# Query heads by way of DRAM, and a top-k search with two small operations a step, in a hybrid attention and mLSTM block

## The chip, the cores and the metric

The kernel runs on one core of a Trainium2 chip. The metric is device time in microseconds (us) from launch to end; lower is better. The engines of a core are TensorE (PE, matrix products), VectorE (DVE), ScalarE (ACT), GpSimd (POOL) and SyncE (SP), which here issues the DMAs. Each engine works through its own instructions in order.

## What is computed

One layer of a streaming encoder on 1024 tokens of width 1024: half a SwiGLU network, then a mixing stage with sparse attention and an mLSTM side by side, then half a second SwiGLU network. The part that the change touches is the attention's indexer (`iq`, `ik`), its top-k and the main queries (`aq`):

```python
h = rms_norm(x, mix_norm[l])
(aq, ak, av, iq, ik, iw, mx, mv, mi, mf, mo, ga, gb) = split_columns(h @ w_in[l])
q = rms_norm(aq.reshape(B, S, ATT_HEADS, ATT_HEAD_DIM), q_norm[l])
...
logits = jnp.einsum('bqhd,bsd->bqhs', iq_blk, ik)
score = jnp.einsum('bqhs,bqh->bqs', jax.nn.relu(logits), iw_blk).astype(jnp.float32) * idx_scale
...
top_s, top_i = lax.top_k(score, k_sel)
...
s = jnp.einsum('bqgrd,bqkgd->bqgrk', q_blk, kg).astype(jnp.float32) * att_scale
p = jax.nn.softmax(s, axis=-1).astype(vg.dtype)
```

There are 8 indexer heads and 8 attention heads of 64 columns each, query blocks of 128, and the 256 best keys of a query are kept.

## The kernel before

All products are in float32, made from pairs of rounded halves: a value is split into `hi` (a ScalarE copy to a rounded type) and `lo` (a VectorE subtraction, value minus `hi`), and `mm3` (L784 to L790) sums three products of halves. The large products save one multiplication in eight by a scheme of seven products of sums per pair of 256 weight columns; a result comes out as "corners" (p, y, th): pair p of columns, half y of the pair (128 columns on the partitions, so two heads of 64), half th of the tokens (512). VectorE writes a corner from PSUM (L1224, L1256, L1261), and `done()` hands it to its user.

The stages are: first feed-forward network up to about 640 us; indexer queries and keys (pairs IQ0, IQ1 and `ik`) 700 to 742; `scores` 742 to 800; the gates, the mLSTM's inputs, the top-k search and the mLSTM 847 to 1094; the last pairs (MO, AKV, and AQ0, AQ1, the main queries) up to about 1180; `proj_b` (the mLSTM's output projection, L1934 to L1954) and attention from then on; the second network from about 1500 to the end. The list MIXING sets the order of the products; `pump` lays those of the mixing projection between the work of scores, search and mLSTM, and calls what was put off with `later`. Within this a scheduler orders each engine's instructions when the kernel is built, so that an edit can also move instructions of lines that it does not touch.

An attention product wants a head's 64 columns of `hi` and `lo` one above the other on the 128 partitions, so that one matmul sums over both. `heads_T` makes these tiles from a corner: two half-height copies on ScalarE and two half-height subtractions on VectorE, since the two heads of a corner end on different halves of the partitions. Its tiles are `iqT` for the indexer and `aqT` for attention. The corners of IQ1 are stored to DRAM (`d_iq`) and fetched inside `scores`, which works through the head pairs j = 0 to 3 with two heads each, six query blocks per head: two matmuls (L1471, L1472), a Relu on ScalarE (L1501) and a weighted sum on VectorE (L1504, L1506).

The search for the 256th best score works on the bits of the float, highest first, for four query blocks at once (384, 512, 640 and 768 keys wide); the two widest blocks have a search of their own on ScalarE (L1610). Each of 31 steps of `search_counts` sets a bit in a candidate (L1582), counts for each block the scores that reach it (L1584, four wide operations), compares the counts with the wanted number (L1586), and takes the bit over where there were enough (L1587).

A corner of the main queries goes through `queries`: `heads_T` into `aqT`, the squares for the norm on ScalarE (L2038), and sums of them on TensorE with the matrix `headsel` (L2043). The segment `swap`, in which `aqT` lies, is free only after product (AQ1, 4), when a hook calls `sums_used`; corners that come earlier wait in `aq_wait` until then. `attn_k` turns keys with TensorE transposes (L2022). Then attention's query-key products (again `qk`, L1471 and L1472) are laid among those of `proj_b`.

## Time and profile before

| what | value |
|---|---|
| time, median of three runs | 2110.75 us |
| lowest and highest of the three | 2107.24 and 2111.69 us |
| the profiled execution's own time | 2112.66 us |
| its span, first to last instruction | 2110.9 us |
| TensorE busy | 2044.5 us, 97% |
| VectorE busy | 1652.0 us, 78% |
| ScalarE busy | 1054.4 us, 50% |
| GpSimd busy | 381.7 us, 18% |
| DMA, mean over the span | 160 GB/s |

Busy times come from one profiled execution. Matmuls are pipelined and their ends are modelled, so a busy TensorE need not be at its peak; the distance from one matmul's start to the next says more. Idle time of an engine matters only where another one waits for it. Line numbers (L1584) are those of the kernel before.

### The profile page before, as it was taken

Reading aid. Unit: us, or ns where it says so; the run is one execution under the profiler, and the core shown is the slowest. Engines: PE = TensorE matmul, PEld = TensorE weight load, DVE = VectorE, ACT = ScalarE, POOL = GpSimd, SP = SyncE. Lnnn points to the kernel's source line nnn. Section 1 sums busy time; section 2 is a strip of 40 time slices with the busy share of each in tenths; the row PEclk is TensorE's granted clock in tenths of the full one; section 3 lists DMA queues with packets and bytes.
Section 4 is the critical chain, followed back from the end, with each engine's and each line's share of the span. In section 5 each row is a group of like instructions: output and inputs, shape, how many; then the busy total and the mean of one; then the engine's idle time right before and its main releaser. Section 6 shows DMA issues by size and latency. Waiting matters only on the chain.

```text
span 2110.9 us, 27903 instructions
## 1 busy us (share of the span) xinstructions
PE 2044.5 (97%) x9349; PEld 1675.8 (79%) x9349; DVE 1652.0 (78%) x2852; ACT 1054.4 (50%) x1968; POOL 381.7 (18%) x397
## 2 busy tenths in 40 slices
PE   7999999999999989999998999899999999999999
PEld 5788888888787778677776888688888888888887
DVE  7988888678866785998979789797976666669963
ACT  8332323334346564885786578735633333334442
POOL 1000000000304323343445545412000000000300
PEclk9999999999999999999999999999999999999999
DMA  5488894493723223365586312742343333377341
GB/s 185 140 283 281 268 303 135 145 381 124 234 103 132 79 73 107 105 185 173 175 271 208 122 54 71 251 153 90 105 138 108 97 103 106 104 286 257 95 141 40
DMA packets 284107, 338.30 MB, mean 160 GB/s; under 512 B 21196, under 2 KB 186684, under 8 KB 283964
## 3 DMA queue, kind: packets, MB, share of 16 engines
q1 hardware_dynamic: 283964, 336.53, 49.0%
q8 instruction: 73, 1.20, 0.2%
q14 instruction: 70, 0.57, 0.1%
HBM read 231.57 MB, written 104.89 MB: 159 GB/s over the span
## 4 chain that ended last, share of the span: by engine, by line
PE 77%; DVE 11%; DMA 5%; ACT 3%; issue 3%; POOL 1%; SPq 0%; DVEq 0%; ACTq 0%; POOLq 0%
PE psum L789 23%; PE psum L788 23%; PE psum L790 23%; DVE plain L1584 2%; PE psum L1472 1%; PE psum L1471 1%; PE psum L2091 1%; DVE h L918 1%; PE psum L2146 1%; PE psum L2145 1%; DMA plain<-d_tb 1%; PE psum L900 1%; DMA raw<-in_ffn_w_up_dram 0%; ACT plain L1501 0%; ACT plain L1610 0%
## 5 line engine op out<-in xcount | busy, mean ns | idle before, releaser
L788 PE MATMUL psum<-h,round 128*128 128x512 f32 x656 | 261.1, 399 | 1.6 <-ACT more L1222 1.0
L789 PE MATMUL psum<-h,round 128*128 128x512 f32 x656 | 260.0, 397 | 1.0 <-DVE h L918 0.8
L790 PE MATMUL psum<-h,round 128*128 128x512 f32 x656 | 259.1, 396 | 1.2 <-POOL round L531 0.9
L667 POOL TENSOR_TENSOR swap<-swap,h 128x1024 f32<-128x1024 f32 x12 | 32.9, 2773 | 1012.1 <-DVE h L653 507.1
L531 POOL TENSOR_TENSOR round<-raw,round 128x512 fp32r<-128x512 f32 x108 | 151.9, 1413 | 146.0 <-ACT round L530 105.8
L790 PEld LDWEIGHTS psum<-h,round 128*128 128x128 f32 x656 | 124.2, 189 | 28.9 <-issue 1.6
L788 PEld LDWEIGHTS psum<-h,round 128*128 128x128 f32 x656 | 124.2, 189 | 28.5 <-ACT more L1222 1.4
L789 PEld LDWEIGHTS psum<-h,round 128*128 128x128 f32 x656 | 124.4, 190 | 27.1 <-DVE h L918 1.5
L788 PE MATMUL psum<-swap,round 128*128 128x512 f32 x328 | 130.9, 400 | 5.8 <-ACT swap L917 2.1
L789 PE MATMUL psum<-swap,round 128*128 128x512 f32 x328 | 129.6, 395 | 2.1 <-DVE swap L918 1.9
L790 PE MATMUL psum<-swap,round 128*128 128x512 f32 x328 | 129.1, 394 | 0.0
L1584 DVE TENSOR_SCALAR_CACHE_REDUCE plain<-plain 128x384 bf16<-128x384 f32 (+1 forms) x124 | 100.4, 809 | 2.5
L297 ACT ACTIVATE round<-plain 128x512 fp32r<-128x512 f32 x79 | 49.6, 633 | 99.2 <-PE psum L789 77.9
L917 ACT ACTIVATE round<-plain 128x512 fp32r<-128x512 f32 x74 | 46.2, 631 | 97.7 <-PE psum L789 90.8
L530 ACT ACTIVATE round<-raw 128x512 fp32r<-128x512 f32 x108 | 66.6, 623 | 29.0 <-PE psum L789 15.4
L790 PE MATMUL psum<-side 128*128 128x512 f32 x208 | 80.9, 389 | 0.0
L789 PE MATMUL psum<-side 128*128 128x512 f32 x208 | 80.9, 389 | 0.0
L788 PE MATMUL psum<-side 128*128 128x512 f32 x208 | 80.9, 389 | 0.0
L789 PE MATMUL psum<-h,spare 128*128 128x512 f32 x200 | 78.2, 391 | 1.9 <-DVE h L918 1.9
L788 PEld LDWEIGHTS psum<-swap,round 128*128 128x128 f32 x328 | 62.3, 190 | 22.0 <-ACT swap L917 2.4
L788 PE MATMUL psum<-h,extra 128*128 128x512 f32 x200 | 77.9, 390 | 1.6 <-DVE plain L1224 1.6
L788 PE MATMUL psum<-h,spare 128*128 128x512 f32 x200 | 78.4, 393 | 0.4 <-ACT h L917 0.4
(740 smaller groups left out, 5975.1 us busy)
## 6 DMA issues: line engine op xcount, KB each, us to landing
plain<-d_a SPq DMA_DIRECT2D x154, 256.0 KB
d_a<-plain SPq DMA_DIRECT2D x123, 256.0 KB
raw<-in_ffn_w_gate_dram SPq DMA_DIRECT2D x44, 512.0 KB
raw<-d_s SPq DMA_DIRECT2D x74, 256.0 KB
h<-in_ffn_w_down_dram SPq DMA_DIRECT2D x66, 256.0 KB
plain<-in_w_in_dram SPq DMA_DIRECT2D x29, 512.0 KB
d_s<-plain SPq DMA_DIRECT2D x58, 256.0 KB
raw<-in_w_in_dram SPq DMA_DIRECT2D x53, 256.0 KB
```

What stands on the lines that cost most here:

```text
L297: k.nc.scalar.activation(hi.r.rearrange("p (k c) -> p k c", k=4), src, AF.Copy)
L530: self.done_A = k.nc.scalar.activation(hi.r, raw.f, AF.Copy).ins
L531: k.nc.gpsimd.tensor_tensor(lo.r, raw.f, hi.f, ALU.subtract)
L667: k.nc.gpsimd.tensor_tensor(x(th, dh), x(th, dh), u, ALU.add)
L788: mm(ps, lhs[0], rhs[0], start=start, stop=False, skip_group_check=more)
L789: mm(ps, lhs[0], rhs[1], start=False, stop=False, skip_group_check=more)
L790: mm(ps, lhs[1], rhs[0], start=False, stop=stop, skip_group_check=more)
L900: self.nc.tensor.transpose(ps[:, i * P:(i + 1) * P], xn[i].f[:, k * P:(k + 1) * P], self.ident)
L917: self.split_A = self.nc.scalar.activation(hi, src, AF.Copy).ins
L918: self.nc.vector.tensor_tensor(lo, src, hi.bitcast(F32), ALU.subtract)
L1471: self.nc.tensor.matmul(o, qb, khi.r[:, s * n:s * n + n], start=True, stop=False)
L1584: v.tensor_scalar(s.junk[:, :s.width[j]], s.sc[j], s.cand[:, j:j + 1], None, ALU.is_ge, ALU.add, accum_out=s.cnt[:, j:j + 1])
```

## The change

It has three parts.

1. **Search.** The wide counting operation starts its sum at minus the wanted number (a second scalar per partition, `s.neg`), so that the sign of the count is the decision. A step then has two small operations: one makes the bit from the sign, one clears it where there were too few and sets the next bit. `cand` starts as 2.0, whose only set bit is the highest.
2. **Indexer heads.** Only the corners of pair IQ0's first half still go through `heads_T`. The other six go through the new `halves_out`: one full-height copy, one full-height subtraction, and two stores of 128x512 to DRAM. `heads_back` fetches a head pair with four DMAs of 64x1024, each half at its place.
3. **Main queries.** All eight corners go through `halves_out`, as soon as they are made; `queries_now` and `aq_wait` are gone, and `sums_used` only gives `swap` its new use. When both token halves of a pair are there, `heads_back` fetches it three steps later.

```diff
-            self.heads_T(self.iqT, y, th, c.f, self.iq_home)
-            c.free()
-        elif p == IQ1:
-            dma(self.d_iq[y, :, cs], c.f)
-            c.free()
+        if p in (IQ0, IQ1):
+            if p == IQ0 and y == 0:
+
+                self.heads_T(self.iqT, 0, th, c.f, self.iq_home)
+                c.free()
+            else:
+                self.halves_out(self.d_iq[2 * p + y - 1], th, c, c)
...
+    def halves_out(self, d, th, c, lo):
+
+        nc = self.nc
+        cs = slice(th * 512, th * 512 + 512)
+        hi = self.rr.alloc(512)
+        nc.scalar.activation(hi.r, c.f, AF.Copy)
+        nc.vector.tensor_tensor(lo.r, c.f, hi.f, ALU.subtract)
+        for i, t in enumerate((hi, lo)):
+            nc.sync.dma_start(d[i, :, cs], t.f)
+            t.free()
+
+    def halved(self, what):
+
+        self.both[what] = what in self.both
+        return self.both[what]
+
+    def heads_back(self, heads, d):
+
+        for e, t in enumerate(heads):
+            for i in range(2):
+                self.nc.sync.dma_start(t.f[i * 64:i * 64 + 64], d[i, e * 64:e * 64 + 64, :])
...
-            if 0 < j < 3:
-
-                for th in range(2):
-                    t = ar.alloc(512)
-                    nc.sync.dma_start(t.f, self.d_iq[j - 1, :, th * 512:th * 512 + 512])
-                    self.heads_T(self.iqT, j + 1, th, t.f, self.iq_home)
-                    t.free()
+            if j < 3:
+
+                self.iqT[j + 1] = self.iq_home(), self.iq_home()
+                self.heads_back(self.iqT[j + 1], self.d_iq[j])
...
-        v.memset(s.pref, 0.0)
+        one = lambda c, j: c[:, j:j + 1]
+        v.tensor_scalar(s.neg, s.kk, -1.0, None, ALU.mult)
+
+        v.memset(s.cand, 2.0)
         for bit in range(30, -1, -1):
-            v.tensor_scalar(i32(s.cand), i32(s.pref), 1 << bit, None, ALU.bitwise_or)
             for j in range(s.n):
-                v.tensor_scalar(s.junk[:, :s.width[j]], s.sc[j], s.cand[:, j:j + 1], None, ALU.is_ge, ALU.add,
-                                accum_out=s.cnt[:, j:j + 1])
-            v.tensor_tensor(i32(s.keep), s.cnt, s.kk, ALU.is_ge)
-            v.copy_predicated(i32(s.pref), i32(s.keep), i32(s.cand))
+
+                v.tensor_scalar(s.junk[:, :s.width[j]], s.sc[j], one(s.cand, j), one(s.neg, j), ALU.is_ge, ALU.add,
+                                accum_out=one(s.cnt, j))
+            v.tensor_scalar(i32(s.up), s.cnt, 0.0, float(1 << bit), ALU.is_lt, ALU.mult)
+            if bit:
+
+                v.scalar_tensor_tensor(i32(s.cand), i32(s.up), 1 << bit - 1, i32(s.cand), ALU.bitwise_or, ALU.bitwise_xor)
+            else:
+                v.tensor_tensor(i32(s.pref), i32(s.up), i32(s.cand), ALU.bitwise_xor)
             yield
...
-        if self.aq_wait is not None:
-            self.aq_wait.append((j, th, c))
-            return
...
-        self.heads_T(self.aqT, j, th, c.f, lambda: self.take("swap", 1024))
+        self.halves_out(self.d_aq[j], th, c, ar.alloc(512))
...
-    def queries_now(self):
-        self.segment("swap", None)
-        wait, self.aq_wait = self.aq_wait, None
-        for w in wait:
-            self.queries(*w)
+        if self.halved(("aq", j)):
+            self.aqT[j] = self.take("swap", 1024), self.take("swap", 1024)
+            self.later(3, lambda: self.heads_back(self.aqT[j], self.d_aq[j]))
```

What an engine issues in which order is shown at three places. In these rows a name is that of the tile, out<-in, and "x4" stands for as many alike in a row; the lines of the changed kernel are its own (its L1607 is L1584 of before, L1609 and L1612 the two small operations of a step, L2066 and L2049 are L2043 and L2022, L1494 and L1495 are L1471 and L1472, L1473 and L1485 the DMAs of `halves_out` and `heads_back`, L1969 is L1942).

VectorE, the last step of the search, before:

```order
L1587 COPY_PREDICATED plain<-plain 128x4
L1582 TENSOR_SCALAR plain<-plain 128x4
L1584 TENSOR_SCALAR plain<-plain 128x384
L1584 TENSOR_SCALAR plain<-plain 128x512
L1584 TENSOR_SCALAR plain<-plain 128x640
L1584 TENSOR_SCALAR plain<-plain 128x768
L1586 TENSOR_TENSOR plain<-plain 128x4
L1587 COPY_PREDICATED plain<-plain 128x4
```

VectorE, a step near the end of the search in the changed kernel:

```order
L1609 TENSOR_SCALAR plain<-plain 128x4
L1612 SCALAR_TENSOR_TENSOR plain<-plain 128x4
L1607 TENSOR_SCALAR plain<-plain 128x384
L1607 TENSOR_SCALAR plain<-plain 128x512
L1607 TENSOR_SCALAR plain<-plain 128x640
L1261 TENSOR_TENSOR more<-more,psum 128x512
L1607 TENSOR_SCALAR plain<-plain 128x768
L1927 SCALAR_TENSOR_TENSOR more<-more,par_651 128x512
L1224 TENSOR_TENSOR plain<-more,psum 128x512
L1609 TENSOR_SCALAR plain<-plain 128x4
L1224 TENSOR_TENSOR plain<-more,psum 128x512
L1612 SCALAR_TENSOR_TENSOR plain<-plain 128x4
```

Between the wide operations of one step and the next stand two small ones instead of three; products' corners (L1224, L1261) lie among them in both.

TensorE at the start of attention, before; the two groups of `proj_b` products (`psum<-h`) around the key transposes are 12 matmuls each, and a further 12 stand ahead of these, so that 36 follow the last product of the queries:

```order
L790 MATMUL psum<-h_8419,round 128x512
L788 MATMUL psum<-h_8419,round 128x512
L789 MATMUL psum<-h_8419,round 128x512
L790 MATMUL psum<-h_8419,round 128x512
L2022 MATMUL psum<-ident,plain 128x128 x8
L788 MATMUL psum<-h_8419,round 128x512
L789 MATMUL psum<-h_8419,round 128x512
L790 MATMUL psum<-h_8419,round 128x512
```

TensorE at the same place in the changed kernel; 12 matmuls of `proj_b` follow the last product of the queries, of which these are the last four:

```order
L790 MATMUL psum<-h_8411,round 128x512
L788 MATMUL psum<-h_8411,round 128x512
L789 MATMUL psum<-h_8411,round 128x512
L790 MATMUL psum<-h_8411,round 128x512
L2066 MATMUL psum<-headsel,plain 128x2 x4
L2066 MATMUL psum<-headsel,spare 128x2 x4
L2049 MATMUL psum<-ident,plain 128x128 x16
L1494 MATMUL psum<-side,swap 128x512
L1495 MATMUL psum<-side,swap 128x512
L1494 MATMUL psum<-side,swap 128x512
```

The transposes, all 16 together, and attention's first products (`psum<-side,swap`) now follow the first 12 `proj_b` matmuls; the other 24 come later.

SyncE at the end of the query products, before (`d_tb` holds what `proj_b` is added to, `raw` are weights):

```order
L865 DMA raw<-in_w_proj_b_dram 128x4x128
L1942 DMA plain<-d_tb 128x512
L865 DMA raw<-in_w_proj_b_dram 128x4x128
L865 DMA raw<-in_w_proj_a_dram 128x4x128
L865 DMA raw<-in_w_proj_b_dram 128x4x128
L1942 DMA h_8690<-d_tb 128x512 x9
L865 DMA raw<-in_w_proj_a_dram 128x4x128 x2
```

SyncE at the same place in the changed kernel:

```order
L1485 DMA swap<-d_aq 64x1024 x5
L1473 DMA d_aq<-round 128x512
L1473 DMA d_aq<-plain 128x512
L1485 DMA swap<-d_aq 64x1024 x3
L1473 DMA d_aq<-round 128x512
L1473 DMA d_aq<-spare 128x512
L1485 DMA swap<-d_aq 64x1024 x4
L1969 DMA plain<-d_tb 128x512
L1485 DMA swap<-d_aq 64x1024 x4
L1969 DMA plain<-d_tb 128x512
L1969 DMA h_8681<-d_tb 128x512 x4
```

The fetches of the heads (`swap<-d_aq`) and the last four stores (`d_aq<-...`) stand ahead of all but the first of the `d_tb` loads of this place; before, only weights stood among these.

## Rows read from the trace of the kernel before

**Rows 1.** The page: the chain that ended last, shares of the span by engine.

```profile
PE 77%; DVE 11%; DMA 5%; ACT 3%; issue 3%; POOL 1%; SPq 0%; DVEq 0%; ACTq 0%; POOLq 0%
```

**Rows 2.** Five stretches: from:to and length (us), busy us and count by engine, granted clock, DMA.

```profile
700.00:742.00 42.00, 37.26 (x168) 29.62 (x168) 34.21 (x40) 20.90 (x34) 15.30 (x10) 0.99 0.32 96
742.00:800.00 58.00, 52.34 (x235) 42.76 (x235) 49.12 (x54) 41.12 (x61) 14.23 (x10) 0.97 0.24 73
847.00:1094.00 247.00, 234.32 (x1161) 186.62 (x1160) 219.57 (x568) 193.98 (x465) 102.29 (x92) 1.00 0.59 172
1151.00:1186.60 35.60, 32.91 (x166) 26.84 (x164) 33.34 (x49) 25.20 (x44) 24.69 (x16) 0.98 0.40 121
1184.90:1195.30 10.40, 9.11 (x31) 7.79 (x31) 4.18 (x12) 0.92 (x2) 10.25 (x7) 0.52 0.94 304
```

**Rows 3.** VectorE's groups by line, 847 to 1094 us: count, busy us, mean ns, idle before.

```profile
L1584 DVE TENSOR_SCALAR_CACHE_REDUCE plain<-plain 128x384 bf16<-128x384 f32 (+1 forms) x124 | 100.4, 809 | 2.5
L1582 DVE TENSOR_SCALAR plain<-plain 128x4 int32<-128x4 int32 x31 | 10.3, 333 | 0.7
L1586 DVE TENSOR_TENSOR plain<-plain 128x4 int32<-128x4 f32 x31 | 9.7, 313 | 0.4
L1587 DVE COPY_PREDICATED plain<-plain 128x4 int32<-128x4 int32 x31 | 9.1, 293 | 0.7
```

**Rows 4.** Line L1582 alone: least, median and longest ns, first and last start.

```profile
L1582 DVE TENSOR_SCALAR plain<-plain x31: 150/171/1267, 852.1 to 1089.7; 128x4 int32<-128x4 int32 x31
```

**Rows 5.** Chain of work, 847 to 1094 us: shares by line, and two pieces.

```profile
by line: DVE plain L1584 13.5%; issue 8.6%; DMA plain<-d_tb 5.0%; PE psum L788 4.8%; PE psum L790 4.7%; PE psum L789 4.6%; ACT plain L1610 2.7%; DVE plain L1582 2.2%; DMA spare<-d_w 2.1%; DMA spare<-d_h 2.0%; DMA d_tb<-plain 2.0%; DVE extra
...
1077.62 4.99 DMA d_tb<-plain
1082.62 5.29 DMA plain<-d_tb
```

**Rows 6.** VectorE's plain scalar operations of 128x896, by shape, 990 to 1141 us.

```profile
L1633 DVE TENSOR_SCALAR plain<-plain 128x896 f32<-128x896 f32 x1 | 0.7, 734 | 0.0
...
L1562 DVE TENSOR_SCALAR plain<-plain 128x896 f32<-128x896 f32 x1 | 0.7, 683 | 0.0
```

**Rows 7.** Chain of work, 742 to 800 us: shares by line.

```profile
by line: PE psum L1471 18.1%; PE psum L1472 16.7%; ACT plain L1501 12.8%; PE psum L788 10.9%; PE psum L789 10.6%; DVE plain L1506 10.3%; PE psum L790 9.8%; issue 5.0%; DVE extra L1462 2.9%; DVE spare L1461 1.2%; DVE rawx L1224 1.2%; ACT spa
```

**Rows 8.** VectorE's groups, 742 to 780 us: half-height and full-height subtractions.

```profile
L1461 DVE TENSOR_TENSOR round<-rawx,round 64x512 fp32r<-64x512 f32 x2 | 1.4, 685 | 0.1
L1224 DVE TENSOR_TENSOR rawx<-plain,psum 128x512 f32<-128x512 f32 x2 | 1.4, 684 | 0.0
```

**Rows 9.** ScalarE's groups, 742 to 780 us: one full-height copy.

```profile
L530 ACT ACTIVATE more<-raw 128x512 fp32r<-128x512 f32 x3 | 1.9, 630 | 0.2 <-PE psum L789 0.2
```

**Rows 10.** TensorE in order of time, around the start of attention: start us, us.

```profile
1180.02 0.40 PE L790 MATMUL psum<-h,round 128*128 128x512 f32 x1
1180.25 0.39 PE L788 MATMUL psum<-h,round 128*128 128x512 f32 x1
...
1182.31 0.95 PE L2043 MATMUL psum<-headsel,plain 128*128 128x2 f32 x8
1183.12 0.49 PE L788 MATMUL psum<-h,round 128*128 128x512 f32 x1
...
1186.25 3.58 PE L2043 MATMUL psum<-headsel,more 128*128 128x2 f32 x16 [1.29 <-DVE plain L2046]
...
1194.95 1.31 PE L2022 MATMUL psum<-ident,plain 128*128 128x128 f32 x8
...
1198.85 0.62 PE L1471 MATMUL psum<-side,swap 128*128 128x512 f32 x2
```

**Rows 11.** SyncE's queue in order of time: DMA issues of one line.

```profile
1183.43 4.51 SPq L1942 DMA_DIRECT2D h<-d_tb  x9
```

**Rows 12.** DMA traffic, 1140 to 1200 us: bytes, and share of 16 engines.

```profile
DMA packets 9506, 9.21 MB, mean 153 GB/s; under 512 B 544, under 2 KB 6688, under 8 KB 9504
...
q1 hardware_dynamic: 9504, 9.18, 49.6%
```

More of the change, by code (lines that the diff above doesn't have):

```diff
@@ L1352, in done @@
         cs = slice(th * 512, th * 512 + 512)
-        if p == IQ0:
-            self.heads_T(self.iqT, y, th, c.f, self.iq_home)
-            c.free()
-        elif p == IQ1:
-            dma(self.d_iq[y, :, cs], c.f)
-            c.free()
+        if p in (IQ0, IQ1):
[4 more added lines that the diff above has]
+                self.halves_out(self.d_iq[2 * p + y - 1], th, c, c)
         elif p in GATES:
@@ L2272, in run @@
         self.d_tb = self.dr.tile([8, P, S], F32, name="d_tb")
-        self.d_iq = self.dr.tile([2, P, S], F32, name="d_iq")
+        self.d_iq = self.dr.tile([3, 2, P, S], F32, name="d_iq")
+        self.d_aq = self.dr.tile([4, 2, P, S], F32, name="d_aq")
         self.d_q = self.dr.tile([8, 4, 64, P], F32, name="d_q")
@@ L2311, in run @@
         self.iqT, self.iq_home = {}, lambda: self.rr.alloc(1024, keep=True)
-        self.aqT, self.aq_wait, self.kn, self.kn_half, self.vs = {}, [], None, 0, None
+        self.aqT, self.both, self.kn, self.kn_half, self.vs = {}, {}, None, 0, None
         T = self.T
@@ L2326, in sums_used @@
             used(5, 4)
-            self.queries_now()
+            self.segment("swap", None)
         self.hooks = {(AQ1, 1): first_used, (AQ1, 4): sums_used, (AQ1, 2): lambda: used(6, 2, 3),
```

## Prediction

> **What bounds the kernel now.** I read the page first. TensorE makes 77% of the chain that ended last, VectorE 11%, DMA 5% [rows 1]. So the change, which touches no product of TensorE, can only win back what TensorE loses while it waits for others, and this has to be read from the stages the change touches. The table of stretches [rows 2] names them: 700 to 742 us (products of the indexer's queries), 742 to 800 (scores), 847 to 1094 (top-k search beside the mixing projection and mLSTM), 1151 to 1186.6 and 1184.9 to 1195.3 (the last queries and attention's start). In each TensorE is idle for some of the time, but VectorE is the fuller of its helpers: 219.57 of 247 us in the third, 33.34 of 35.6 in the fourth. In the last the granted clock is 0.52, the lower of the two levels (1.2 and 2.4 GHz), and the DMA share 0.94.
>
> **The change, part by part.** The profiled execution took 2112.66 us (its span 2110.9 and 1.8 around it). It stands 1.9 above the median of the three runs, 2110.75. The sum is made against 2112.66.
>
> *Search.* Each of 31 bits loses one of three small operations (L1582, L1586, L1587). They took 10.3, 9.7 and 9.1 us for 31 each [rows 3], so one is 0.313 us on average and 31 of them are 9.7 us of VectorE. An undisturbed one is 0.171 (the median), a few are over 1.2 [rows 4]; at the median the 31 are 5.3 us. The saving counts only where VectorE is what TensorE waits for. The chain of this stretch puts 13.5% of 247 us = 33 us on L1584, of 100.4 us busy (a third), and 2.2% = 5.4 us on L1582, of 10.3 (half) [rows 3, 5]. I take 0.41, between: **-4.0 us**. The bounds are 0 (something else ends the waits) and -9.7.
>
> A small operation's price can be read otherwise. The Trainium skill, "VectorE: DVE Perf Modes", section "The TRN2 errata", gives an operation on SBUF 58 cycles plus its columns at 0.96 GHz, so 0.065 us for four columns: by that estimate the 31 would be 2.0 us and the term -0.8. The trace does not bear this out: no L1582 took less than 0.150. The section's second figure, a measured fixed term of about 150 cycles (0.156 us), agrees.
>
> The wide operation L1584 gets a second scalar per partition, which no counting operation of the trace has. The nearest rows are plain ones of 128x896: 734 ns with two such scalars (L1633), 683 with one (L1562) [rows 6]. So 0 to 51 ns more, for 124 of them 0 to 6.3 us of VectorE; I take half, 3.1, and L1584's third of the chain: **+1.0** (0 to +2.1).
>
> *Scores.* Eight half-height copies and eight half-height subtractions (`heads_T` for j = 2 and 3) leave the stretch 742 to 800. The chain has 2.9% of it on L1462 and 1.2% on L1461 [rows 7], 4.1% of 58 us: **-2.4**. The bounds are 0 and the 5.7 us for which TensorE isn't busy there [rows 2]. In place of the operations come DMAs, twelve stores and twelve loads of 256 KB. What hides them is the work on the head pair before: a quarter of the 58 us, 14.5, against a store and a load behind each other, 4.99 + 5.29 = 10.3 us in the chain's rows [rows 5]. Were that cover gone, each of three pairs could cost up to 10.3.
>
> *Indexer's queries, 700 to 742.* The splitting moves here: four half operations each on ScalarE and VectorE go and six full ones come. A full-height one costs what a half-height one did (subtraction 0.69 and 0.68 [rows 8]; copy 0.63 [rows 9]), so VectorE gets 1.4 us more, with 34.21 of 42 us busy [rows 2]. Half of that: **+0.7** (0 to +1.4).
>
> *Main queries.* Sixteen half operations on each of two engines become eight full ones, about 5.5 us less on VectorE and 5 on ScalarE, and the first corners no longer wait. Against that stand 32 DMAs of 256 KB, 8.4 MB. What it is worth is read at TensorE's end of the stage [rows 10]. Now: the last product of the queries starts at 1180.02 (counted back from the headsel rows by the order), so T = 1180.25, where `proj_b` begins, is its end, and attention's first qk starts at 1198.85, 18.6 us later. Between them stand 36 matmuls of `proj_b` at 0.23 us, 32 small ones with headsel at 0.1 (eight in 0.81) and 8 transposes, 1.31 as a group and about 0.9 without the low clock (an estimate): 12.4 us at full clock. Lost: 6.2 us, of which 1.29 is the wait in front of 1186.25 and some 5 the low clock behind it (48% of 10.4 us, [rows 2]).
>
> After: the order shows only 12 matmuls of `proj_b`, 32 with headsel and 16 transposes before that qk, 2.8 + 3.2 + 1.8 = 7.8 us of cover. Its operands come by DMA: corner, copy and subtraction of the last product take 0.68 + 0.63 + 0.68 = 2.0 us, and behind them SP issues two stores and the two loads of the first head at 0.5 each (4.51 us for nine [rows 11]). With a landing of 5 us, as in [rows 5], the head is there at T + 9.0 to 9.3; with one of under 3.8 it isn't waited for. So idle time is 0 to 1.5 us, and I take 1.5. A wait of 1.29 brought the low clock here; a like wait may do so again, so I add half its price, 2.5. Lost 4.0 instead of 6.2: **-2.2**. The bounds are -6.2 (no wait, full clock) and the rival below.
>
> The Trainium skill, "DMA: Bandwidth & Descriptors", section "Anatomy of one DMA — SWDGE (gpsimd) path", speaks against such a detour: a DMA pays about 2.0 us besides its bytes at 436 GB/s, most of it the receipt of the write, worst for HBM. It was fitted to DMAs issued by GpSimd; these are SP's. By that estimate one landing is 2.6 us and store plus load 5.2, half of the 10.3 in this trace. The first head would then be there at T + 6.6, inside the cover, and the tail, with the same half price of the low clock, would gain 3.7.
>
> Sum: -4.0 + 1.0 - 2.4 + 0.7 - 2.2 = **-6.9**, so 2105.8 against the profiled execution and 2103.9 against the median. I predict 2104.
>
> **Rivals.** *More than that.* VectorE is the limit wherever it is on the chain, and the tail never waits: -9.7 + 1.0 - 2.4 + 0.7 - 6.2 = -16.6, 2096 (2094 by the median). For it: VectorE has hardly a gap from 1151 to 1186.6. Against it: TensorE was idle for only 12.7 us of the 247, and DMA and ScalarE end some of those waits.
>
> *No change.* The search's time goes to the next wait in line. The same chain holds loads and stores of d_tb at about 5 us each and ScalarE's own search, L1610, with 2.7% [rows 5]; these don't move. The tail's new wait with its low clock (1.5 + 5) makes up the 6.2 won. Left are -2.4 and +0.7: 2111 (2109 by the median).
>
> *Slower.* The DMA engines fill at attention's start. From 1140 to 1200 they move 9.21 MB, at half their time [rows 12]; 8.4 more make 17.6 MB in 60 us, 293 GB/s, against 304 at a share of 0.94 [rows 2]. Then two stores and four loads (1.57 MB) take 5.2 us ahead of a landing of 5.3: first head at T + 12.5, 4.7 us of idle and 5 of low clock, 3.5 more than the 6.2 now. And the nine d_tb loads, which the evacuation of `proj_b` needs, stand on SP behind eight loads and two stores, 2.6 MB or 8.6 us later than now. In all +12.1 in the tail and -4.7 elsewhere: +7.4, 2120 (2118 by the median). It turns the result to slower once the tail costs 8.9 us. For it: the share of 0.94 where the nine loads run. Against it: from 1151 to 1186.6 the share is only 0.40, and most stores and loads belong to earlier corners.
>
> **How the numbers follow.** A measurement of this kernel tells about 0.2%, 4.2 us, from no change, so faster means under 2106.5. The forecast (2099 to 2108) gets 0.48, the larger gain 0.12, no change 0.23, slower 0.17. The first two are faster, which makes 0.60; 0.23 same; 0.17 slower. The range leaves out the ends of the larger gain and the upper part of the slower rival: 2096 to 2117. The forecast's own is 2099 to 2108.
>
> **What would show it.** The 31 steps should show two small operations each, with VectorE's busy time from 847 to 1094 some 7 us lower; if the wide operation is over 30 ns longer at 128x768 than now, the second scalar costs. The scores should have neither L1461's kind of row nor waits of TensorE behind it. At attention's start, the time from the last query product to the first qk should be about 12 us, with less than 2 us of wait for a load of `heads_back` or for a copy behind a store. The prediction fails if the search stretch is no shorter though its operations are gone, or if TensorE waits over 4 us for DMA around the first heads.

## The result and the profile after

The changed kernel is slower: 2127.2 us in the median (four runs, 2124.2 to 2130.41) against 2111.22 (2107.24 to 2113.2), a ratio of 1.0078 [1.0057, 1.0099]. The forecast was 2104, the range up to 2117. The profiled execution took 2130.41 us, its span is 2128.7, 17.8 more than before. The rows below are in the order of the groups ahead of the prediction; line numbers are those of the changed kernel.

The page's chain that ended last, by engine (answers to [rows 1]):

```profile
PE 67%; DVE 14%; DMA 9%; issue 4%; ACT 3%; POOL 1%; SPq 1%; DVEq 0%; POOLq 0%; ACTq 0%
```

TensorE gives up 10 points of the chain, most of them to DMA (5% to 9%) and VectorE (11% to 14%). The stretches (from:to and length, busy us and count by engine, granted clock, DMA share and GB/s; answers to [rows 2], the last two moved to where these stages now lie):

```profile
700.00:742.00 42.00, 37.60 (x169) 29.87 (x168) 36.19 (x51) 24.45 (x38) 17.04 (x11) 0.99 0.41 132
742.00:800.00 58.00, 53.65 (x246) 44.13 (x245) 44.34 (x53) 38.13 (x56) 13.95 (x9) 0.97 0.48 127
847.00:1094.00 247.00, 237.19 (x1168) 191.72 (x1167) 215.50 (x504) 183.84 (x452) 104.30 (x92) 0.99 0.59 171
1151.00:1190.00 39.00, 35.60 (x148) 29.49 (x148) 26.11 (x39) 19.01 (x33) 21.05 (x12) 0.82 0.52 178
1196.00:1212.00 16.00, 10.28 (x39) 7.73 (x39) 8.29 (x14) 6.41 (x9) 8.54 (x7) 0.59 1.04 265
```

Up to 800 us the kernel does as forecast: TensorE is busy 53.65 us in the scores, 1.31 more than before, and VectorE 44.34 instead of 49.12. The bad stretches are the last two: a clock of 0.82, where the kernel before has 0.94 over the same 39 us, and at the start of attention a DMA share of 1.04 with TensorE idle for 5.7 of 16 us (before: 0.94, and 1.3 of 10.4).

VectorE's groups by line, 847 to 1094 us (count, busy us, mean ns, idle before; answers to [rows 3]):

```profile
L1607 DVE TENSOR_SCALAR_CACHE_REDUCE plain<-plain 128x384 bf16<-128x384 f32 (+1 forms) x124 | 107.7, 869 | 2.1
L1612 DVE SCALAR_TENSOR_TENSOR plain<-plain 128x4 int32<-128x4 int32 x30 | 12.5, 416 | 0.7
L1609 DVE TENSOR_SCALAR plain<-plain 128x4 int32<-128x4 f32 x31 | 10.7, 346 | 0.4
```

The small operations fell from 29.1 us [rows 3] to 23.2, and the wide ones rose from 100.4 to 107.7: the search costs VectorE 130.9 us instead of 129.5. The same wide operation with its shapes kept apart, first after, then before:

```profile
L1607 DVE TENSOR_SCALAR_CACHE_REDUCE plain<-plain 128x768 bf16<-128x768 f32 x31 | 33.1, 1067 | 0.4
...
L1607 DVE TENSOR_SCALAR_CACHE_REDUCE plain<-plain 128x384 bf16<-128x384 f32 x31 | 20.7, 669 | 0.6
```

```profile
L1584 DVE TENSOR_SCALAR_CACHE_REDUCE plain<-plain 128x768 bf16<-128x768 f32 x31 | 31.3, 1008 | 0.4
...
L1584 DVE TENSOR_SCALAR_CACHE_REDUCE plain<-plain 128x384 bf16<-128x384 f32 x31 | 18.9, 610 | 0.7
```

59 ns more at both ends of the width. TensorE in order of time around the start of attention (start us, us; the bracket is idle time before and what ended it; answers to [rows 10]):

```profile
1190.51 0.39 PE L790 MATMUL psum<-h,round 128*128 128x512 f32 x1
1190.74 0.95 PE L2066 MATMUL psum<-headsel,more 128*128 128x2 f32 x8
...
1200.59 1.97 PE L2049 MATMUL psum<-ident,plain 128*128 128x128 f32 x8 [3.44 <-DVE plain L2069]
1203.27 1.97 PE L2049 MATMUL psum<-ident,plain 128*128 128x128 f32 x8 [0.71 <-DVE side L2051]
1206.44 0.77 PE L1494 MATMUL psum<-side,swap 128*128 128x512 f32 x1 [1.19 <-DMA swap<-d_aq]
1207.00 0.63 PE L1495 MATMUL psum<-side,swap 128*128 128x512 f32 x1
```

From the end of the last query product (T = 1190.74) to the first attention product pass 15.7 us, with three waits that make 5.3 us. Before it was 18.6, but 24 more products of `proj_b` (5.5 us) lay inside. What TensorE waits for stands on VectorE and ScalarE at the same time, each held by a store that has not landed. VectorE, then ScalarE:

```profile
1198.59 1.87 DVE L2042 COPY plain<-plain 128x512 f32<-128x512 f32 x2 [3.61 <-DMA d_aq<-plain]
```

```profile
1197.88 0.63 ACT L185 ACTIVATE round<-raw 128x512 fp32r<-128x512 f32 x1 [2.99 <-DMA d_aq<-round]
```

The key copies (L2042) and a weight's rounding (L185) want the buffers that `halves_out` has just filled and that stay taken until their store is through. SyncE's queue there (answers to [rows 11]), and one of its own waits, 1195 to 1205 us:

```profile
1192.37 0.58 SPq L1473 DMA_DIRECT2D d_aq<-round  x1
1193.05 0.38 SPq L1473 DMA_DIRECT2D d_aq<-plain  x1
...
1197.92 2.39 SPq L1485 DMA_DIRECT2D swap<-d_aq  x4
1202.40 0.33 SPq L1969 DMA_DIRECT2D plain<-d_tb  x1
1203.52 2.39 SPq L1485 DMA_DIRECT2D swap<-d_aq  x4
1206.32 0.33 SPq L1969 DMA_DIRECT2D plain<-d_tb  x1
1207.47 3.69 SPq L1969 DMA_DIRECT2D h<-d_tb  x4
```

```profile
SPq L1485 <- DMA d_aq<-round: 2.0, 2, 1.2
```

The `d_tb` loads, at 1183.43 before, come at 1202 to 1211. The first attention product needs the first two of the four loads of 1197.92, which fetch what the stores of 1192.37 and 1193.05 wrote. In the trace's records of landings (the same that give the 4.99 and 5.29 us of [rows 5]) these stores land at 1197.85 and 1198.57, 5.5 us after their issue; SyncE issues the two loads only then, at 1197.92 and 1198.58, and they land at 1205.20 and 1206.30, 7.3 and 7.7 us later. So a store and a load stand behind each other, 13 us together, ahead of the product at 1206.44.

**Where the time went.** For a picture over the whole span I gave each matmul of a trace the usual distance from its start to the next (by shape), summed these as work done, and compared when two executions reach the same work. Positive is late against the kernel before, in us; the columns are places at the kernel before's times. The rows without an edit ahead of a place show how exact it is: about 1 to 2 us. The kernels are those of the next section.

| kernel | 890 | 1050 | 1070 | 1150 | 1170 | 1190 | 1220 | 1400 |
|---|---|---|---|---|---|---|---|---|
| after | -5.5 | -10.2 | -2.0 | 0.5 | 8.2 | 8.3 | 12.8 | 15.5 |
| search_only | 1.7 | -0.6 | 7.1 | 6.5 | 9.1 | 10.6 | 8.4 | 7.4 |
| old_search_new_order | 2.0 | 0.2 | 7.8 | 6.6 | 11.2 | 9.8 | 8.8 | 8.0 |
| search_held | 1.3 | 1.9 | 2.8 | 3.9 | 3.8 | 3.8 | 3.8 | 4.2 |
| indexer_only | -5.1 | -8.5 | -7.7 | -8.8 | -3.1 | -4.6 | -5.1 | -3.0 |
| queries_only | -0.2 | 0.7 | 0.7 | 1.3 | 4.4 | 3.3 | 10.4 | 11.2 |
| before_plus_traffic | 0.2 | -0.5 | 0.1 | 1.1 | 2.1 | 0.8 | 7.9 | 7.3 |
| queries_direct | 0.4 | 0.0 | 0.6 | 0.6 | 0.6 | -2.5 | -0.8 | 0.4 |

The changed kernel is ahead until 1050, loses 8 us within the next 20, 8 between 1150 and 1170, and 4.5 between 1190 and 1220. The first and last of these have experiments below.

### The profile page after: what moved, and what is told of

Read it like the earlier page. It is cut to its first block, busy times and chain, and to the rows that moved or that the text cites. A ratio compares the mean times of both kernels' runs of the same rounds, so it can differ in the third digit from the quotient of the medians.

```text
span 2128.7 us, 27931 instructions
## 1 busy us (share of the span) xinstructions
PE 2054.8 (97%) x9349; PEld 1684.3 (79%) x9349; DVE 1642.3 (77%) x2808; ACT 1041.6 (49%) x1951; POOL 380.7 (18%) x397
## 4 chain that ended last, share of the span: by engine, by line
PE 67%; DVE 14%; DMA 9%; issue 4%; ACT 3%; POOL 1%; SPq 1%; DVEq 0%; POOLq 0%; ACTq 0%
PE psum L789 20%; PE psum L788 20%; PE psum L790 20%; DVE plain L1607 1%; PE psum L1494 1%; DMA plain<-in_w_in_dram 1%; PE psum L1495 1%; PE psum L2111 1%; DMA more<-in_w_in_dram 1%; DMA swap<-d_aq 1%; DMA raw<-in_ffn_w_gate_dram 1%; PE psum L2166 1%; DMA raw<-in_w_in_dram 1%; POOL round L531 1%; PE psum L900 1%
## 5 line engine op out<-in xcount | busy, mean ns | idle before, releaser
L789 PE MATMUL psum<-swap,round 128*128 128x512 f32 x328 | 130.9, 399 | 0.7 <-DVE swap L918 0.5
L1607 DVE TENSOR_SCALAR_CACHE_REDUCE plain<-plain 128x384 bf16<-128x384 f32 (+1 forms) x124 | 107.7, 869 | 2.1
L788 PE MATMUL psum<-h,spare 128*128 128x512 f32 x208 | 81.6, 394 | 2.2 <-DVE plain L1080 1.1
L789 PE MATMUL psum<-h,spare 128*128 128x512 f32 x208 | 81.3, 391 | 1.9 <-DVE h L918 1.9
L918 DVE TENSOR_TENSOR round<-plain,round 128x512 fp32r<-128x512 f32 x74 | 54.7, 745 | 32.5 <-ACT round L917 32.4
```

What stands on the lines that cost most here:

```text
L788: mm(ps, lhs[0], rhs[0], start=start, stop=False, skip_group_check=more)
L789: mm(ps, lhs[0], rhs[1], start=False, stop=False, skip_group_check=more)
L918: self.nc.vector.tensor_tensor(lo, src, hi.bitcast(F32), ALU.subtract)
L1607: v.tensor_scalar(s.junk[:, :s.width[j]], s.sc[j], one(s.cand, j), one(s.neg, j), ALU.is_ge, ALU.add, accum_out=one(s.cnt, j))
```

## The experiments

The kernel before ran beside each group: 2112.38 us in the median (17 runs) for the first four, 2112.95 (21) for the next four, 2113.58 (27) for the last four.

**One part at a time.** Three kernels have one part of the change each, and a fourth only the second scalar of the wide operation, as a zero.

`search_only`: the kernel before with the diff of `search_counts` (the change's first part).

> The kernel before with the change's search alone (two small operations, second scalar on the wide one). Theory 1, the second scalar costs what the small operation saved: the wide operations take some 7 us more of VectorE in all and the small ones 6 less, so the time stays within 3 us of before, 2109 to 2114 us. Rival, the search does save and the loss comes from the queries: 3 to 5 us faster, 2106 to 2108 us.

Measured: 2122.1 us, 1.005 [1.0035, 1.0065]. Neither theory gave it: +10 us with one operation a step less. The wide operation is as long as in the changed kernel, which eats up the small operations' saving but doesn't explain ten more.

`indexer_only`: the diff's edits to `done` for IQ0 and IQ1 and to `scores`, with `halves_out` and `heads_back`.

> The kernel before with the indexer's heads by way of DRAM alone. Theory 1: the scores stretch is 2 to 3 us shorter, nothing else moves, 2107 to 2109 us. Rival: the DMAs hold SP's queue and the weight loads behind them, and what the scores win is lost by 850 us, 2110 to 2114 us.

Measured: 2108.76 us, 0.9984 [0.9975, 0.9994], so 3.5 us won. The stretch of the scores, of this kernel:

```profile
742.00:800.00 58.00, 53.65 (x246) 44.37 (x247) 44.23 (x51) 38.01 (x55) 13.95 (x9) 0.98 0.47 126
```

It is the changed kernel's row to the hundredth of TensorE, so this part does there what it does alone.

`queries_only`: the diff's edits to `queries`, `queries_now` and `sums_used`.

> The kernel before with the main queries' part alone (not held back, by way of DRAM). Theory 1, nearly all of the loss is here: from 1140 us to the first qk the kernel loses 10 to 14 us, 2121 to 2126 us, with VectorE's key copies (L2015) waiting 3 us or more for a store of d_aq to land. Rival, the loss at 1050 us (mLSTM) and the one at 1150 us come from the altered order of search and indexer: at most 6 us slower, 2111 to 2117 us.

Measured: 2123.36 us, 1.0054 [1.0042, 1.0066]. The stretches of the start of attention (columns as above), and TensorE's row for the first attention product:

```profile
1190.00:1200.00 10.00, 5.77 (x33) 4.45 (x31) 3.45 (x9) 4.03 (x7) 4.70 (x4) 0.76 1.06 285
1200.00:1212.00 12.00, 9.75 (x35) 7.38 (x36) 5.97 (x11) 4.68 (x7) 6.03 (x7) 0.77 1.04 211
```

```profile
1201.86 0.76 PE L1493 MATMUL psum<-side,swap 128*128 128x512 f32 x1 [2.43 <-DMA swap<-d_aq]
```

The DMA engines are full for 22 us, TensorE is idle for 6.5 of them at a low clock. ScalarE's L185 again waited for `d_aq<-round`, 4.5 us in two waits. The time is that of Theory 1, but not by its sign: VectorE's key copies have no wait for a store here.

`zero_scalar`: the kernel before, whose wide operation starts its sum at a scalar that is zero.

```diff
+        v.memset(s.neg, 0.0)
...
-                v.tensor_scalar(s.junk[:, :s.width[j]], s.sc[j], s.cand[:, j:j + 1], None, ALU.is_ge, ALU.add,
+                v.tensor_scalar(s.junk[:, :s.width[j]], s.sc[j], s.cand[:, j:j + 1], s.neg[:, j:j + 1], ALU.is_ge, ALU.add,
```

> The kernel before, whose wide counting operation gets a second scalar per partition that is zero; nothing else is changed and the three small operations stay. Theory 1, the scalar's price is the instruction's own: each of the four widths is 55 to 65 ns longer than before (768 columns: 1.06 instead of 1.01 us), 7 us more of VectorE, 2 to 5 us slower, 2113 to 2116 us. Rival, the longer wide operations after the change come from what runs beside them: 1.01 us as before, and 2109 to 2112 us.

Measured: 2135.79 us, 1.0109 [1.0092, 1.0125]. The wide operations took 1064 ns at 768 columns and 670 at 384, so a zero costs what any scalar costs; but 124 times 59 ns are 7.3 us, and the kernel lost 23. Something else came with the edit. The order of instructions, beside that of the kernel before, shows what: the scheduler that orders each engine at build time had moved others too. Counted by the longest common sequence of the two traces, 288 of TensorE's 9,349 matmuls and 157 of VectorE's 2,852 instructions stand out of the old order.

**Edit and order apart.** In the next three kernels a list written into the kernel holds every engine to a given order: each instruction gets a dependency on the one ahead of it on its engine, of a kind that puts no wait into the program.

```diff
+    for engine, order in _orders().items():
...
+                tc.add_manual_dep(i, last.name, mybir.DependencyInfo(mybir.DependencyClass.NoSync,
+                                  mybir.DependencyReason.DATA), reason="held")
```

`scalar_held` is zero_scalar in the order of the kernel before; `search_held` is search_only in it (the dropped operations left out of the list); `old_search_new_order` has the instructions of the kernel before in the order of search_only.

> The kernel with the zero second scalar again, but every engine's instructions are held in the order of the kernel before (the one memset apart). Theory A, the altered order made most of its 23 us: the wide operations are 59 ns longer as they were, 7.3 us in all, a third of which counts, so 2112 to 2117 us. Theory B, VectorE's time is simply worth that much there: 2127 us or more, as without the held order.

> The change's search alone, with every engine's instructions held in the order of the kernel before (the dropped small operations left out). Theory A, the altered order is what cost search_only 10 us: without it 7.3 us of longer wide operations stand against 6 to 9 us of dropped small ones, 2108 to 2114 us. Theory B: 2119 us or more, as without the held order.

> The kernel before, its three small operations and its single scalar kept, but every engine's instructions held in the order that search_only had. Theory A: the order alone costs, 2117 to 2125 us. Theory B: the order is harmless, 2108 to 2114 us.

Measured: scalar_held 2115.77 us, 1.002 [1.001, 1.0029]; search_held 2115.69, 1.0012 [1.0002, 1.0022]; old_search_new_order 2125.13, 1.0059 [1.0047, 1.0072]. So the second scalar costs some 4 us of the 23, and the whole search edit 2.5 us of its ten (0.4 to 4.6 by the interval). The new order without the new search costs all that search_only cost. (search_held and old_search_new_order lie just above their ranges of Theory A.)

In search_held the two small operations that stay cost less than in the changed kernel (847 to 1100 us):

```profile
L1589 DVE TENSOR_SCALAR plain<-plain 128x4 int32<-128x4 f32 x31 | 9.7, 313 | 0.4
L1592 DVE SCALAR_TENSOR_TENSOR plain<-plain 128x4 int32<-128x4 int32 x30 | 8.7, 289 | 0.6
```

They take 10.7 us less than the three of before (18.4 against 29.1), and the wide ones are 7.3 longer, as everywhere with the second scalar. The search thus keeps VectorE busy for 3.4 us less than before, and the kernel is no faster; why it is rather slower, no run shows.

**Where the order costs.** The table of lateness puts the cost of the order at one place, 1050 to 1070: 7.7 us in search_only, 7.6 in old_search_new_order, 8.2 in the changed kernel, 0.9 in search_held. VectorE's waits, 1000 to 1065 us (line waited for: us in total, times, longest), in turn after, before, old_search_new_order and search_held:

```profile
DVE more L1861 <- DMA raw<-d_s: 6.0, 1, 6.0
```

```profile
DVE more L1834 <- issue: 2.1, 1, 2.1
```

```profile
DVE more L1834 <- DMA raw<-d_s: 5.2, 1, 5.2
```

```profile
DVE more L1841 <- DMA more<-d_w: 1.6, 1, 1.6
```

It is one operation of the mLSTM, which multiplies with a vector fetched from `d_w`. (The row names a load of `d_s`; what it multiplies is the load that SyncE had issued at 1044.30, in the changed kernel's queue.) In the new orders VectorE stands in front of it for 5 to 6 us, and TensorE behind VectorE; of the changed kernel:

```profile
1052.83 2.07 PE L1843 MATMUL psum<-plain 128*128 128x128 f32 x8 [4.52 <-DVE rawx L1883]
```

In old_search_new_order the same wait is 4.0 us; the kernel before has none over 1.1 from 1040 to 1085. The two stretches around it (columns as above), of the kernel before, then of old_search_new_order:

```profile
1040.00:1060.00 20.00, 18.80 (x102) 15.30 (x101) 17.59 (x47) 13.20 (x36) 8.55 (x7) 1.00 0.47 142
1060.00:1080.00 20.00, 19.64 (x96) 15.96 (x95) 12.38 (x33) 18.98 (x47) 9.68 (x8) 1.00 0.71 225
```

```profile
1040.00:1060.00 20.00, 16.00 (x91) 13.02 (x90) 14.56 (x41) 15.36 (x42) 8.43 (x9) 0.96 0.50 145
1060.00:1080.00 20.00, 19.81 (x100) 17.35 (x99) 15.16 (x46) 11.45 (x27) 4.66 (x4) 0.87 0.61 174
```

TensorE is idle for 4.2 of these 40 us instead of 1.6, and behind the wait its clock is lower, 0.96 and 0.87 where it was 1.00. By an estimate from these shares (0.04 and 0.13 of 20 us) the clock takes another 3.4 us; idle time and clock together make 6.0 of the 7.6.

**What it is in the main queries.** `queries_hi_apart` is queries_only with `hi` in a slot of its own, so that the rounding of weights no longer waits for its store.

```diff
-        hi = self.rr.alloc(512)
+        hi = self.ar.alloc(512)
```

> queries_only, but the hi half of a corner lies in the general buffers and no longer in those in which weights are rounded. Theory H, ScalarE's rounding of weights (L185) behind a store's landing makes the loss: its waits for d_aq stores, 1.9 and 2.6 us there, are gone and the time is 2112 to 2118 us. Theory D, the full DMA engines at the first heads make it: the first qk still waits over 2 us for a load of heads and the time stays at 2119 us or more.

Measured: 2123.24 us, 1.0054 [1.0041, 1.0067], no better. L185's wait is gone, and TensorE waits for the loads instead:

```profile
1198.34 0.77 PE L1493 MATMUL psum<-side,swap 128*128 128x512 f32 x1 [5.39 <-DMA swap<-d_aq]
```

So the slot of `hi` is not what costs here; the loads land too late with or without it. (The `lo` half was left in its slot.)

`before_plus_traffic` is the kernel before, in its own order, with the bytes of the detour added and nothing that waits for them: after each finished corner two stores of 256 KB, after each pair four copies of 256 KB from DRAM to DRAM.

```diff
...
+        for i in range(2):
+            dma(self.d_aq[j, i, :, cs], self.aqT[j][i].f[:, cs])
+        if self.both.setdefault(j, 0):
+            for e in range(4):
+                dma(self.d_junk[j, e % 2, e // 2 * 64:e // 2 * 64 + 64, :], self.d_aq[j, e % 2, e // 2 * 64:e // 2 * 64 + 64, :])
```

> The kernel before, every engine held in its order, and beside its own work the change's traffic of the main queries: 16 stores of 256 KB of the finished heads to DRAM and 16 copies of 256 KB of these into a DRAM tile that nobody reads. No product waits for them. Theory D1, it is the round trip on the way to the first product that costs: without that dependence the time stays at 2110 to 2115 us. Theory D2, the traffic itself and SP's queue behind it cost: 2118 us or more, with loads of d_tb and weights landing late.

Measured: 2121.14 us, 1.004 [1.0024, 1.0057]. Its longest wait for a DMA, 1140 to 1230 us, and TensorE's row behind it:

```profile
DVE h L1949 <- DMA h<-d_tb: 9.7, 1, 9.7
```

```profile
1201.50 0.80 PE L788 MATMUL psum<-h,round 128*128 128x512 f32 x1 [7.40 <-DVE h L1949]
```

SyncE's queue in this kernel:

```profile
1190.95 3.08 SPq L2038 DMA_DIRECT2D d_junk<-d_aq  x4
...
1195.24 1.12 SPq L1942 DMA_DIRECT2D h<-d_tb  x2
1196.40 1.10 SPq L2038 DMA_DIRECT2D d_junk<-d_aq  x2
1197.63 3.37 SPq L1942 DMA_DIRECT2D h<-d_tb  x5
```

Nobody reads the added bytes, and still 7.6 us are lost, nearly all at one place (0.8 late at 1190, 7.9 at 1220): the `d_tb` loads stand behind them on SyncE, land late, VectorE's evacuation of `proj_b` (L1949) waits, and TensorE behind it. This is a price of the traffic in the order of before, with 36 products of `proj_b` ahead of attention. In the changed kernel 24 of these come later, and TensorE has no wait there behind an evacuation of `proj_b`; in queries_only it has two, 0.37 and 1.33 us.

`queries_direct` keeps the corners waiting as the kernel before does, and has the full-height copy and subtraction, but no DRAM: four DMAs for each corner carry the halves from SBUF to SBUF.

```diff
-        self.heads_T(self.aqT, j, th, c.f, lambda: self.take("swap", 1024))
...
+        nc.scalar.activation(hi.r, c.f, AF.Copy)
+        v.tensor_tensor(lo.r, c.f, hi.f, ALU.subtract)
+        for e, t in enumerate(self.aqT[j]):
+            for i, half in enumerate((hi, lo)):
+                nc.sync.dma_start(t.f[i * 64:i * 64 + 64, cs], half.f[e * 64:e * 64 + 64])
```

> The kernel before, whose main queries are split at full height and then moved by four DMAs of 64x512 from SBUF to SBUF per corner (128 KB each), still held back as before: no DRAM, half the bytes. Theory D1, the round trip costs: with one landing instead of two the first qk waits 1 to 3 us and the time is 2108 to 2116 us. Theory D2, 32 more DMAs and their place in SP's queue cost: 2118 us or more.

Measured: 2112.14 us, 0.9998 [0.9988, 1.0009]. From 1140 to 1220 us the DMA engines moved 14.45 MB, against 10.29 before and 17.69 in queries_only, and the loss is gone. Its DMA engines are as full as those of queries_only, with TensorE busy throughout (columns as above):

```profile
1190.00:1200.00 10.00, 10.00 (x40) 8.09 (x39) 5.24 (x10) 4.43 (x6) 0.83 (x3) 0.82 1.05 323
```

So full engines alone are not the loss. The kernel has one landing where the detour has two, and half of its bytes, and it holds the corners back; which of these counts most was not taken apart. A gain is not to be seen either: eight operations saved on each of two engines, with 32 small DMAs in their place, are worth nothing here that can be measured.

`queries_held_back` is queries_only with the hold of before, corners waiting in `aq_wait` until product (AQ1, 4):

```diff
-            self.segment("swap", None)
+            self.segment("swap", None)
+            wait, self.aq_wait = self.aq_wait, None
+            for w in wait:
+                self.queries(*w)
```

> queries_only (by way of DRAM), but the first corners wait for the hook as before. If not holding them back helps the round trip to start early, this is slower than queries_only: the first qk waits 2 to 6 us longer, 2125 to 2130 us. Rival: the early corners are what crowds SP's queue and ScalarE around 1150 us (3 us there), and with the hold the time is 2112 to 2121 us.

Measured: 2119.69 us, 1.0038 [1.0024, 1.0052]. With the hold it is some 3.5 us faster than queries_only, but the two intervals overlap. The early start of the first corners, which the change brought, is not seen to help; that it costs is likely and not shown.

`indexer_and_queries_direct` joins indexer_only and queries_direct and leaves the search as before.

> indexer_only and queries_direct together, with the search of before. If the parts add up, the time is that of queries_direct less 3.6 us: 2104 to 2113 us by D1. Rival: the order of the instructions comes out otherwise with both, and costs as search_only's did, 2115 to 2122 us.

Measured: 2105.91 us (11 runs), 0.9973 [0.9962, 0.9984]: faster than both kernels.

## Why the prediction was wrong

The three parts alone give +0.50, -0.16 and +0.54%, +0.88% in all; the whole gave +0.78%. These agree within their intervals, so the parts are judged one by one. Each of the three kernels also has an order of its own, and only that of the search was held fixed.

**What bounds the kernel.** The stages were the right ones: all that was won or lost lies in them or right behind them.

**Search (forecast -4.0 + 1.0, measured +10).** What failed above all is that the sum had no term for the order: the document ahead of the prediction says that an edit can move instructions of lines it does not touch, and the working priced the moved rows nowhere. They cost +0.59% alone (old_search_new_order), more than any term of the sum.

The step that turned VectorE's time into the kernel's failed as well. The small operations' saving was well sized for the old order (forecast 9.7 us, search_held 10.7; in the changed kernel, among other neighbours, it is 5.9). The second scalar was bounded at 0 to 51 ns from plain operations of another kind [rows 6] and is 58 to 60: the bound was no bound. With these sizes the prediction's shares of the chain (0.41 and a third) give -4.4 + 2.4 = -2.0 us, and search_held measured +2.5. A share of the chain did not tell what a shorter operation is worth.

**Scores and indexer's queries (-2.4 + 0.7, measured -3.5).** Right in mechanism, and larger than forecast. The rows of the half-height subtraction are gone from the scores, TensorE's waits there for ScalarE's Relu (before: 5.6 us, after: 4.4) shrank, and the loads were hidden by the head pair before, as costed. The interval is -5.3 to -1.3 us (0.9975 and 0.9994 of 2112), and the forecast, -1.7, lies in it. The 3.5 are a net sum, though: the table has this kernel 5.1 us ahead at 890 and 8.5 at 1050, and 5.7 of these go again between 1150 and 1170, outside the stages of this part. The order of indexer_only was not held, so what of this is the operations and what the order stays open.

**Main queries (-2.2, measured +11.4).** The step that failed is "with a landing of 5 us ... the head is there at T + 9.0 to 9.3". It counts one landing, the load's. The load reads from DRAM what a store has to write there first, and SyncE issues it only when that store has landed; in the scores the prediction itself put a store and a load behind each other, 10.3 us. With both its working would give T + 14.0 to 14.3. By the prediction's cover of 7.8 us that is some 6.5 us idle instead of 1.5, and with the half price of the low clock the term is +2.8 instead of -2.2. The first product came at T + 15.7, released by that load, with a store of 5.5 and a load of 7.7 us in front. So the store's landing, 5.5 us, is the larger part of the miss, and the load's longer landing, 7.7 instead of 5 where the DMA share is 1.04, the smaller. A second thing was left out: until they land, the stores hold the buffers that VectorE's key copies and ScalarE's rounding want (3.61 and 2.99 us), and TensorE's longest wait, 3.44, is behind these copies.

The slower rival had the late first head (it said T + 12.5, also with one landing and the rest from traffic) and `d_tb` loads pushed back on SyncE. The loads were pushed back, but in the changed kernel, where 24 products of `proj_b` come later, TensorE hardly waited for them; before_plus_traffic shows what they cost where it does, +0.40%. So that its price for the tail, +12.1 us, is close to the 11.4 of queries_only is in part luck. Its weight, 0.17, was too low: the argument against it, a share of 0.40 from 1151 to 1186.6, does not hold where the stores and loads really go, since all 16 loads are issued from 1189 to 1206. The rival's total of 2120 missed for the search alone. That the first corners gain by not waiting is not borne out (queries_held_back).

The estimate from the Trainium skill, "DMA: Bandwidth & Descriptors", section "Anatomy of one DMA — SWDGE (gpsimd) path", T + 6.6, is further off than the rows' 9.3; it too counts one landing, and with the store's the same estimate would be T + 9.2. That section speaks of one DMA; no run here shows one without others around it at this place.

**Signs named ahead.** Those of the scores came out as forecast. The others came out against it: the wide operation is over 30 ns longer, VectorE's busy time from 847 to 1094 us is 4.07 us lower and not 7, and from the last query product to the first attention product it is 15.7 us and not 12. TensorE waits over 4 us around the first heads (3.44 + 0.71 + 1.19): 1.19 of these for a load itself, the 3.44 through VectorE, which stood behind a store.

**What stays open.** The 8 us that the changed kernel loses from 1150 to 1170 have no experiment of their own. TensorE's rows there show two waits, 1.79 us behind ScalarE at 1149.56 and a longer one; below it is GpSimd's row for what that one waited for:

```profile
1162.34 0.80 PE L790 MATMUL psum<-h,round 128*128 128x512 f32 x1 [3.40 <-POOL round L531]
```

```profile
1159.35 4.63 POOL L531 TENSOR_TENSOR round<-raw,round 128x512 fp32r<-128x512 f32 x3 [2.70 <-DMA more<-d_yb]
```

A low clock follows the second (products 0.43 us apart until 1174.9). GpSimd's row names a load of `d_yb`, but the last part of that load landed at 1159.70, when GpSimd had begun. The landing just ahead of its start, at 1159.12, is that of the first store of `halves_out` (issued at 1155.70), which empties one of the buffers that weights are rounded into. In queries_only, which has these stores too, GpSimd's rounding waits 4.2 us in two waits whose rows name them. So the trace points at the early stores of the main queries for this wait; no experiment takes it alone, and queries_hi_apart, which gives `hi` another slot, was no faster. search_only and old_search_new_order lose 2.6 and 4.6 us there too, with no such stores, behind an operation of VectorE (L1256: 2.31 and 3.44 us); queries_only loses 3.1, indexer_only 5.7. How much of the 8 us is the order and how much the stores was not separated.

## What to carry to other kernels

Where a scheduler orders instructions at build time, an edit has two prices, its own and that of the order it brings; hold the order to measure the first, and put the old instructions into the new order to measure the second. A detour through DRAM costs two landings, the store's and then the load's, and holds its source until the first of them: count both from the last operand to the first user. Take their price from the stretch in which the last of them must land, and look at who stands behind them in the issuing queue. A busy time saved is not a time saved: search_held takes 3.4 us off the fullest helper and is no faster.

## What the runs showed of the hardware

- A second scalar per partition on VectorE's accumulating comparison costs 58 to 60 ns an operation at 384, 512, 640 and 768 columns alike (610, 744, 876 and 1008 ns become 669, 802, 936 and 1067), and about as much where it is zero (670, 803, 936 and 1064). At these widths it is a cost per operation, not one per column.
- Traffic that nobody waits for cost 0.40%: 8.4 MB, issued from 1168 to 1202 us, where the DMA share rose from 0.47 to 0.94 (before_plus_traffic).
- DMAs of 256 KB landed 5.5 us (stores) and 7.3 to 7.7 us (loads) after their issue where the DMA share was 1.02 to 1.04; at a share of 0.59 it had been 4.99 and 5.29 [rows 5].
- Small operations of 128x4 took 289 to 416 ns in the mean in the search's stretch (search_held and the changed kernel at the ends), where the shortest of L1582 took 150 [rows 4].
- Around three waits of 3.44, 0.71 and 1.19 us the granted clock was 0.59 over 16 us; attention's products then start 0.43 us apart (1207.00 to 1207.43), the lower of the two levels, where the products before the waits stood 0.23 apart.
